# Turning both groups of the previous tile ahead of a descending tile's own products, and raising three step rates

## The chip, the cores and the metric

One core of one Trainium2 chip. The metric is the device time of one execution in microseconds (us). The kernel before takes 1788.37 us, the median of three runs from 1788.04 to 1789.47.

## What is computed

One layer of a hybrid encoder for two requests with shared weights, a sample of 1024 tokens and a prompt of 256, at model width 2048:

```
hn   = rms_norm(x, norm_g)
proj = hn @ w_in            # xbc, z_ssd, dt, q, k, v, z_att, mq, z_mem
# 1 SSD, 16 heads of 64 in two groups: forward and backward scan over chunks of 128 tokens
y_f  = ssd_scan(xs, dt[0], A[0], B, C)
y_b  = ssd_scan of the same, reversed in time
y    = y_f + y_b + d_skip * xs
o_ssd = rms_norm per group (y * silu(z_ssd))
# 2 attention within a window of 128 tokens, 8 heads, 2 key heads, a sink; gated by z_att
# 3 attention to a memory of 256 entries, 4 heads of 128; gated by z_mem
out  = x + concat(o_ssd, o_att, o_mem) @ w_out
```

All is float32. The step inside one backward chunk that matters here is `y_off = C @ S * exp(acs)`, then `S = S * decay + st`: each tile needs the state that the tile after it in time left behind.

## The kernel before

**Tiles.** The tokens are ten tiles of 128: tiles 0 to 7 are the sample, 8 and 9 the prompt. They are worked in two groups of five, 0 to 4 and 5 to 9. The big products run in blocks, one for a slice of 512 or 256 columns of a weight. A weight chunk is loaded by SP into one of four buffers (`wraw`), split into a high part by ACT (L206, `wh`) and a low part by VectorE (L207, `wl`), and used in three products (L258 to L260 for five tiles at once, `block_tok`; L293 to L295 for features by 320 tokens, `block_feat`). These are the main matmuls, into five PSUM banks called `acc`. TensorE runs them in the order in which they are written.

**Lanes.** All other work is generators in two queues ("lanes"). After each k of a block, `pump(rates)` adds the block's two rates to what each lane is owed and takes whole steps of the lanes by turns; a step is what a generator does up to its next `yield`. `RATES[1]` holds the pair of each block of the second group of tiles, (first lane, second lane); a `block_feat` uses half of it for each k. The first lane holds attention (`attn`) and memory attention (`mem_attn`), the second the ascending and the descending half of the SSD (`ssd_up`, `ssd_down`). `need` takes steps until a named generator is done. So the rates and the number of steps decide beside which main matmuls a step's instructions stand; the engines then run them in a fixed order, each engine its own.

**What the lanes share.** All their products use one pool of three PSUM banks by turns (`pr`, `pd`, `pz`, `pyb`, `psc`, `pms`, `pcb`, `pxs`, `pst` and others), whatever the lane. A new tile waits until the reader of the tile three before it has emptied the bank.

**The descending half.** `ssd_down` runs for tiles 7 to 0 and then 9 and 8. A tile's steps in the kernel before: a first step with its loads by SP (old output `yd`, gate `zd`, state `st`, the turned diagonal part `ydT`), three empty ones (eight more for tiles 7 and 9), then

- the norm of the tile that ran before it (`norm_ssd`, two L1001 on VectorE, which need that tile's `yrs` from POOL), and `diag_in(0)`: four transposes `pd` (L1046) and an add on VectorE (L1047);
- for each of two groups of 512 columns: for the first group of tiles 0 to 4 four transposes `pz` (L1060), then the product with the state `pyb` (L1063), five or six operations on VectorE (L1065 to L1073) and a square on ACT (L1070);
- after each group a step that turns the same group of the tile before (`turn_ssd`: four transposes `pr`, L1010, a copy `so` by ACT, L1012, and a store to `oT` by SP, L1013); after the first group with `diag_in(1)`.

`last_y` hands the output of one tile to the next. Tiles 0 and 8 have no follower and flush their own output at the end: three empty steps, the norm, two empty steps, and two turns.

**What follows from it.** Block `o` (output projection) reads `oT`: at its third k and at its sixth, `fill_direct` loads chunks (`chd`, L188, by SP) of what the SSD stored, and ACT (L200, `xH`) and VectorE (L201) split them. `zm` fills in the same way from the attention outputs (L197 and L198). The loads wait on SP for the stores' landing.

Of the kernel before, what the change touches and what calls it, by code (L numbers as in the profile page):

```python
# [30 lines left out]

RATES = ({'kv': (4.0, 1.0), 'z1': (2.2, 1.7)},
         {'kv': (1.5, 1.5), 'x': (2.1, 2.15), 'q': (2.25, 2.5), 'za': (2.15, 2.5), 'z0': (2.1, 2.5),
          'z1': (2.1, 2.55), 'mq': (2.0, 2.7), 'zm': (1.75, 2.75), 'o': (2.15, 2.4)})
FAR = 1e30

UNITS = (0, 8, 1, 9, 2, 10, 3, 11, 4, 12, 5, 13, 6, 7)
# [7 lines left out]
def hymba_encoder_kernel(  # L45
# [37 lines left out]
    def psum(name):  # L83
        return mix.tile([P, 512], F32, tag="mix", name=name)
# [37 lines left out]
    def rsqrt(dst, src, scale, n):  # L122
        G.tensor_scalar(out=dst, in0=src, scalar1=scale, scalar2=EPS, op0=ALU.mult, op1=ALU.add)
        G.tensor_tensor(out=dst, in0=dst, in1=mhalf[:, :n], op=ALU.pow)

    def hv(ap, n=8):
        return ap.rearrange("p (h d) -> p h d", h=n)

    def hb(ap, n, d):
        return ap.unsqueeze(2).broadcast_to([P, n, d])  # L130
# [673 lines left out]
    def wb(name, dtype=F32, shape=(P, 512)):  # L804
        return mp.tile(list(shape), dtype, tag="wb", name=name, bufs=WBB)
# [190 lines left out]
    def norm_ssd():  # L996

        if "y" in last_y:
            t, ys, rs = last_y.pop("y")
            for g in range(2):  # L1000
                V.tensor_scalar(out=ys[g], in0=ys[g], scalar1=rs[:, g:g + 1], scalar2=None, op0=ALU.mult)  # L1001
                last_y[g] = t, ys[g]

    def turn_ssd(g):

        if g in last_y:
            t, y = last_y.pop(g)
            ps = psum("pr")
            for j in range(4):
                T.transpose(ps[:, j * P:(j + 1) * P], y[:, j * P:(j + 1) * P], ident)  # L1010
            o = mp.tile([P, 512], F32, tag="rb", name="so", bufs=RBB)
            A.activation(o, ps, AF.Copy)  # L1012
            S.dma_start(oT_d[2 + g][t // 5][:, :, t % 5 * P:(t % 5 + 1) * P], hv(o, 4))  # L1013

    def ssd_down(t):
        first = t in (0, NS)
        last = t in (NS - 1, NT - 1)
        tok = slice(t * P, (t + 1) * P)
        ss = sm.tile([P, 2], F32, tag="s2", name="yss", bufs=4)
        if not last:  # L1020
            cc = mp.tile([P, 2, P], F32, tag="btok", name="cc", bufs=1)
            S.dma_start(cc, xbc_d[10:12, :, tok].rearrange("f p c -> p f c"))
        ld = []
        for g in range(2):
            c = slice(g * 512, (g + 1) * 512)

            y = mp.tile([P, 512], F32, tag="ya" if t % 2 else "rf", name="yd", bufs=2)
            S.dma_start(y, yp_d[t][:, c])
            if g == 0 and t < 5:
                z = mp.tile([P, 512], F32R, tag="xs", name="zd", bufs=2)  # L1030
                S.dma_start(hv(z.bitcast(F32), 4), yT_d[:, :, tok])
            else:
                z = mp.tile([P, 512], F32, tag="xs", name="zd", bufs=2)
                S.dma_start(z, z_d[g][t])
            st = None
            if not first:
                st = state[:, c] if last else wb("st2")
                S.dma_start(st, sb_d[t][:, c])
            d = mp.tile([P, 4, P], F32R, tag="rb", name="ydT", bufs=RBB)
            S.dma_start(d.bitcast(F32), yd_d[t][:, 4 * g:4 * g + 4, :])  # L1040
            ld.append((y, z, st, d))

        def diag_in(g):
            ps = psum("pd")
            for j in range(4):
                T.transpose(ps[:, j * P:(j + 1) * P].bitcast(F32R), ld[g][3][:, j, :], identr)  # L1046
            V.tensor_add(ld[g][0], ld[g][0], ps)  # L1047

        for _ in range(9 if last else 4):
            yield  # L1050
        norm_ssd()
        diag_in(0)
        yield
        for g in range(2):
            c = slice(g * 512, (g + 1) * 512)
            y, z, st, _ = ld[g]
            if g == 0 and t < 5:
                zr, z = z, psum("pz")
                for j in range(4):
                    T.transpose(z[:, j * P:(j + 1) * P].bitcast(F32R), zr[:, j * P:(j + 1) * P], identr)  # L1060
            if not last:
                pf = psum("pyb")
                T.matmul(pf, cc[:, g, :], state[:, c], start=True, stop=True)  # L1063
                y2 = wb("y3")
                V.tensor_mul(hv(y2), hv(pf), hb(eacs_all[:, t, 16 + 8 * g:24 + 8 * g], 8, 64))  # L1065
                V.tensor_add(y, y, y2)
            V.tensor_mul(y, y, z)
            if g == 0 and t < 5:
                z = wb("zq")
            A.activation(z, y, AF.Square, scale=0.5, accum_out=ss[:, g:g + 1])  # L1070
            if not first and not last:
                V.tensor_mul(hv(state[:, c]), hv(state[:, c]), hb(cd_all[:, t, 16 + 8 * g:24 + 8 * g], 8, 64))
                V.tensor_add(state[:, c], state[:, c], st)  # L1073
            yield
            turn_ssd(g)
            if g == 0:
                diag_in(1)
                yield
        rs = sm.tile([P, 2], F32, tag="s2", name="yrs", bufs=4)
        rsqrt(rs, ss, 1.0 / 512, 2)  # L1080
        G.tensor_scalar(out=rs, in0=rs, scalar1=0.5, scalar2=None, op0=ALU.mult)
        last_y["y"] = t, [x[0] for x in ld], rs
        yield
        if first:
            for _ in range(3):
                yield
            norm_ssd()
            yield
            yield
            for g in range(2):  # L1090
                turn_ssd(g)
                yield
# [358 lines left out]
    def refill_o(grp, when):  # L1451
        def f(k):
            if k not in when:
                return []
            q = when[k]
            need((attn, mem_attn, ssd_down, ssd_down)[q], range(grp * 5, grp * 5 + 5))
            return [part(fill_direct, q, j, oT_d[q][grp][:, j, :],
                         gain=None if q < 2 else vec[:, R_SG + 4 * (q - 2) + j:R_SG + 4 * (q - 2) + j + 1])
                    for j in range(4)]
        return f  # L1460
# [161 lines left out]
    tok("z0", w_in_rows("z0"), ev_gate(0, 5), grp=1)  # L1622
    tok("z1", w_in_rows("z1"), ev_gate(1, 5), grp=1)
    queue(1, ssd_down, range(7, -1, -1))
    queue(1, ssd_up, range(8, 10))
    queue(1, ssd_down, range(9, 7, -1))
    tok("mq", w_in_rows("mq"), ev_raw(mq_d, 5), grp=1)
    gate("zm", 1, refill_o(0, {3: 0, 7: 1}))
# [100 lines left out]
```

## Time and profile before

| | |
|---|---|
| median of three runs | 1788.37 us |
| the profiled execution | 1792.47 us |
| its span, first to last instruction | 1790.8 us |
| granted TensorE clock | 1.000 |
| TensorE matmul busy | 1776.3 us |
| TensorE weight loads busy | 1605.2 us |
| VectorE, ACT, POOL busy | 1246.8, 921.7, 549.3 us |

Rows of the profile give a start, a duration, the engine and line, and the tile written `<-` the tiles read; "[0.72 <-ACT so L1012]" is the idle of the engine before it and what ended that. Rows of the waits are "total us, times, longest". PE is TensorE's matmuls and PEld its weight loads, which may run under an earlier matmul; matmuls are pipelined and a matmul's end is modelled. Buffer numbers in the order of the program (`pr_14873`) belong to one tile; the lines there are those of the kernel shown, which in the new kernel are two or three higher behind the change.

### The profile page before, as it was taken

How to read it: one execution, taken by the hardware profiler on the slowest of the kernel's cores; microseconds unless marked ns; L12 is line 12 of the kernel's file. 1: busy time of each engine (PE TensorE's matmuls, PEld its weight loads, DVE VectorE, ACT ScalarE, POOL GpSimd, SP SyncE). 2: the span in 40 equal slices, each digit the busy share in tenths (PEclk: the TensorE clock that was granted, in tenths of full speed). 3: DMA queues.
4: the chain of work that ended last, by engine and by line, in shares of the span. 5: the costliest groups of instructions: out<-in, count | busy, mean ns of one | idle time of the engine just before them, and what ended most of it. 6: DMA issues, size and time to landing. Idle time of an engine off the chain costs nothing.

```text
span 1790.8 us, 31435 instructions
## 1 busy us (share of the span) xinstructions
PE 1776.3 (99%) x10838; PEld 1605.2 (90%) x10838; DVE 1246.8 (70%) x2358; ACT 921.7 (51%) x2049; POOL 549.3 (31%) x900
## 2 busy tenths in 40 slices
PE   9999999999999999999999999999999999999999
PEld 7788999999998989999889977877988888899999
DVE  5495788888858878777765676557677644766665
ACT  6554555555434766656454565544447533543332
POOL 0105799998810101010001010000100000057775
PEclk9999999999999999999999999999999999999999
DMA  8663544445446644453635644557777764744442
GB/s 283 198 185 118 146 147 137 146 144 168 123 140 208 187 140 133 147 164 104 188 117 181 187 150 152 170 161 250 225 231 237 239 192 143 223 150 143 148 142 77
DMA packets 208207, 301.12 MB, mean 168 GB/s; under 512 B 19568, under 2 KB 86192, under 8 KB 208048
## 3 DMA queue, kind: packets, MB, share of 16 engines
q1 hardware_dynamic: 207904, 299.06, 54.5%
q8 instruction: 85, 1.39, 0.3%
q14 instruction: 74, 0.61, 0.1%
q10 hardware_dynamic: 144, 0.06, 0.0%
HBM read 236.36 MB, written 62.69 MB: 167 GB/s over the span
## 4 chain that ended last, share of the span: by engine, by line
PE 79%; issue 6%; POOL 5%; DMA 5%; DVE 3%; ACT 2%; SPq 0%; POOLq 0%; ACTq 0%; DVEq 0%
PE acc L258 9%; PE acc L260 9%; PE acc L259 9%; PE acc L1238 6%; PE acc L1236 6%; PE acc L1237 6%; PE acc L293 5%; PE acc L295 5%; PE acc L294 5%; POOL ws L1208 3%; PE accm L1237 2%; PE accm L1236 2%; PE accm L1238 2%; PE po L673 1%; PE ppt L663 1%
## 5 line engine op out<-in xcount | busy, mean ns | idle before, releaser
L207 DVE TENSOR_TENSOR wl<-wraw,wh 128x512 fp32r<-128x512 f32 (+1 forms) x480 | 345.3, 721 | 241.3 <-ACT wh L206 234.0
L206 ACT ACTIVATE wh<-wraw 128x512 fp32r<-128x512 f32 (+1 forms) x480 | 292.0, 613 | 297.4 <-PE acc L260 138.6
L258 PE MATMUL acc<-wh,xH 128*128 128x512 f32 (+1 forms) x1088 | 419.0, 385 | 2.7 <-ACT mkr L420 1.3
L259 PE MATMUL acc<-wl,xH 128*128 128x512 f32 (+1 forms) x1088 | 410.1, 377 | 0.7 <-DVE wl L207 0.7
L260 PE MATMUL acc<-wh,xL 128*128 128x512 f32 (+1 forms) x1088 | 410.2, 377 | 0.0
L258 PEld LDWEIGHTS acc<-wh,xH 128*128 128x128 f32 x1088 | 204.4, 188 | 41.5 <-issue 3.6
L259 PEld LDWEIGHTS acc<-wl,xH 128*128 128x128 f32 x1088 | 204.5, 188 | 38.5 <-DVE wl L207 3.1
L260 PEld LDWEIGHTS acc<-wh,xL 128*128 128x128 f32 x1088 | 204.2, 188 | 36.9 <-issue 0.2
L293 PE MATMUL acc<-xH,wh 128*128 128x320 f32 x640 | 202.7, 317 | 0.0
L206 ACT ACTIVATE sh<-ws 128x384 fp32r<-128x384 f32 x176 | 91.3, 523 | 214.5 <-POOL ws L1208 117.4
L294 PE MATMUL acc<-xL,wh 128*128 128x320 f32 x640 | 198.8, 311 | 0.0
L295 PE MATMUL acc<-xH,wl 128*128 128x320 f32 x640 | 198.0, 309 | 0.0
L207 DVE TENSOR_TENSOR sl<-ws,sh 128x384 fp32r<-128x384 f32 x176 | 124.8, 712 | 104.3 <-ACT sh L206 101.8
L1208 POOL TENSOR_TENSOR ws<-wraw 128x128 f32<-128x128 f32 x176 | 114.1, 648 | 203.8 <-DMA wraw<-in_w_in_pairs_dram 87.7
L635 POOL COPY lg<-nsink 128x2 f32<-128x2 f32 x40 | 14.1, 351 | 377.6 <-PE ppt L663 219.8
L293 PEld LDWEIGHTS acc<-xH,wh 128*128 128x128 f32 x640 | 120.2, 188 | 2.6 <-issue 2.2
L294 PEld LDWEIGHTS acc<-xL,wh 128*128 128x128 f32 x640 | 120.3, 188 | 1.7 <-issue 1.4
L1208 POOL TENSOR_TENSOR ws<-wraw,ws 128x128 f32<-128x128 f32 x176 | 116.7, 663 | 13.8
L295 PEld LDWEIGHTS acc<-xH,wl 128*128 128x128 f32 x640 | 120.2, 188 | 0.6 <-issue 0.5
L1208 POOL TENSOR_TENSOR ws<-ws,wraw 128x128 f32<-128x128 f32 x176 | 116.9, 664 | 0.0
L1208 POOL TENSOR_TENSOR wraw<-wraw 128x128 f32<-128x128 f32 x176 | 111.9, 636 | 13.7
L362 DVE SCALAR_TENSOR_TENSOR c<-u,vec,c 128x638 f32<-128x638 f32 (+1 forms) x96 | 90.0, 938 | 9.0 <-ACT c L357 8.7
(437 smaller groups left out, 3943.3 us busy)
## 6 DMA issues: line engine op xcount, KB each, us to landing
wraw<-in_w_in_laid_dram SPq DMA_DIRECT2D x176, 256.0 KB, 2.9
wraw<-in_w_in_pairs_dram SPq DMA_DIRECT2D x112, 256.0 KB, 2.8
wraw<-in_w_out_laid_dram SPq DMA_DIRECT2D x64, 256.0 KB, 3.3
wraw<-in_w_out_pairs_dram SPq DMA_DIRECT2D x64, 256.0 KB, 2.8
rf<-ac SPq DMA_DIRECT2D x40, 256.0 KB, 4.1
rb<-ac SPq DMA_DIRECT2D x40, 256.0 KB, 4.9
wraw<-in_w_mem_laid_dram SPq DMA_DIRECT2D x32, 256.0 KB, 4.7
xst<-in_x_sample_dram SPq DMA_DIRECT2D x20, 256.0 KB, 4.7
```

Of the source, the lines that this page charges most:

```text
L206: a = A.activation(h, raw, AF.Copy)
L207: b = V.tensor_sub(l, raw, h.bitcast(F32))
L258: T.matmul(ps[t][:, :n], sh, h[:, :n], start=(k_ == 0), stop=False)
L259: T.matmul(ps[t][:, :n], sh, l[:, :n], start=False, stop=False)
L260: T.matmul(ps[t][:, :n], sl, h[:, :n], start=False, stop=(k_ == KT - 1))
L293: T.matmul(o, sh, cur["H", q][:, m, c], start=(k == 0), stop=False)
L294: T.matmul(o, sh, cur["L", q][:, m, c], start=False, stop=False)
L295: T.matmul(o, sl, cur["H", q][:, m, c], start=False, stop=(k == KT - 1))
L1208: G.tensor_tensor(out=o, in0=x, in1=y, op=op)
L1236: T.matmul(ps[p], h, xh, start=(k_ == 0), stop=False)
L1237: T.matmul(ps[p], h, xl, start=False, stop=False)
L1238: T.matmul(ps[p], l, xh, start=False, stop=(k_ == 7))
```

## The change

The turns move from behind each group to a step of their own, ahead of both groups and behind `diag_in(0)`. Three of the rate pairs of the second group of tiles change, so that the second lane takes more steps for each k. A tile then has one step more. Nothing that is computed changes.

```diff
-          'z1': (2.1, 2.55), 'mq': (2.0, 2.7), 'zm': (1.75, 2.75), 'o': (2.15, 2.4)})
+          'z1': (2.1, 2.55), 'mq': (1.95, 3.0), 'zm': (1.75, 3.05), 'o': (2.15, 2.5)})
...
         diag_in(0)
         yield
         for g in range(2):
+            turn_ssd(g)
+        yield
+        for g in range(2):
             c = slice(g * 512, (g + 1) * 512)
             y, z, st, _ = ld[g]
...
                 V.tensor_add(state[:, c], state[:, c], st)
             yield
-            turn_ssd(g)
             if g == 0:
                 diag_in(1)
                 yield
```

TensorE, where tile 4 of the descending half works: before, with the turn of tile 5's first group behind the first product,

```order
L1060 MATMUL pz_14858<-identr_84,zd_14739 128x128 x4
L1063 MATMUL pyb_14863<-state_6124,cc_14735 128x512
L1010 MATMUL pr_14873<-identr_84,yd_14504 128x128 x4
L293 MATMUL acc_14897<-xH0_6806,wh_14902 128x320
L294 MATMUL acc_14897<-xL0_6807,wh_14902 128x320
L295 MATMUL acc_14897<-xH0_6806,wl_14903 128x320
L1046 MATMUL pd_14881<-identr_84,ydT_14751 128x128 x4
```

and now:

```order
L1046 MATMUL pd_14829<-identr_84,ydT_14697 128x128 x4
L293 MATMUL acc_14908<-xH0_6806,wh_14914 128x320
L294 MATMUL acc_14908<-xL0_6807,wh_14914 128x320
L295 MATMUL acc_14908<-xH0_6806,wl_14915 128x320
L673 MATMUL po_14835<-pT_14675,v_all_6118 64x256 x4
L1010 MATMUL pr_14841<-identr_84,yd_14494 128x128 x4
L1010 MATMUL pr_14849<-identr_84,yd_14502 128x128 x4
L293 MATMUL acc_14909<-xH0_6806,wh_14914 128x320
L294 MATMUL acc_14909<-xL0_6807,wh_14914 128x320
L1063 MATMUL pz_14857<-identr_84,zd_14693 128x128 x4
L1066 MATMUL pyb_14862<-state_6124,cc_14689 128x512
```

Both turns (`pr`) stand together ahead of the first product. The second place is tile 0 in block `zm`, on TensorE: before,

```order
L1046 MATMUL pd_15782<-identr_84,ydT_15691 128x128 x4
L1060 MATMUL pz_15790<-identr_84,zd_15689 128x128 x4
L1063 MATMUL pyb_15795<-state_6124,cc_15685 128x512
L293 MATMUL acc_15402<-xH3_7438,wh_15805 128x320
L294 MATMUL acc_15402<-xL3_7439,wh_15805 128x320
```

and now:

```order
L1010 MATMUL pr_15788<-identr_84,yd_15390 128x128 x4
L1010 MATMUL pr_15796<-identr_84,yd_15398 128x128 x4
L1063 MATMUL pz_15804<-identr_84,zd_15677 128x128 x4
L293 MATMUL acc_15412<-xH3_7438,wh_15827 128x320
L294 MATMUL acc_15412<-xL3_7439,wh_15827 128x320
L1066 MATMUL pyb_15809<-state_6124,cc_15673 128x512
L1046 MATMUL pd_15819<-identr_84,ydT_15685 128x128 x4
```

The two turns of tile 1 moved here from 50 rows further down; `pd` of the first group went ahead by a step. Their copies on ACT stand here now:

```order
L197 ACTIVATE xH1_15781<-chd_15735 128x640
L197 ACTIVATE xH1_15781<-chd_15785 128x640
L206 ACTIVATE wh_15921<-wraw_15919 128x512
L722 ACTIVATE sq_15942<-mq_15940 128x512
L1012 ACTIVATE so_15793<-pr_15788 128x512
L1012 ACTIVATE so_15801<-pr_15796 128x512
```

In the old order a square of L1070 followed L722, and the two copies came seven rows later. The third place is ACT at the start of block `o`, where `wh` is a weight split, `mpr` the exps of memory attention and `xH2` the fill with the SSD's chunks: before,

```order
L206 ACTIVATE wh_16187<-wraw_16185 128x512
L754 ACTIVATE mpr_16039,mden_16040<-pms_16029,mm_16036,mr_15946 128x256 x2
L831 ACTIVATE cb_16055<-pcb_16046 128x256
L754 ACTIVATE mpr_16067,mden_16068<-pms_16057,mm_16064,mr_15946 128x256 x2
L200 ACTIVATE xH2_16109<-chd_15986,vec_200 128x640
```

and now:

```order
L206 ACTIVATE wh_16187<-wraw_16185 128x512
L200 ACTIVATE xH2_16109<-chd_15986,vec_200 128x640
L200 ACTIVATE xH2_16109<-chd_16026,vec_200 128x640
L200 ACTIVATE xH2_16109<-chd_16113,vec_200 128x640
L754 ACTIVATE mpr_16039,mden_16040<-pms_16029,mm_16036,mr_15946 128x256 x2
```

The first three fills now come ahead of the first pair of exps.

## The prediction

> **What bounds the kernel now.** I read the page first, then the windows around the descending tiles, then the waits of the matmul engine and of its weight loads there, and last the timelines of the two places that the change packs tighter.
>
> ```profile
> span 1790.8 us, 31435 instructions
> PE 1776.3 (99%) x10838; PEld 1605.2 (90%) x10838; DVE 1246.8 (70%) x2358; ACT 921.7 (51%) x2049; POOL 549.3 (31%) x900
> ```
>
> TensorE is the bound over the whole program: 1776.3 of 1790.8 us. The change adds no arithmetic, so it can only move the remaining idle. The next view cuts the part in which tiles 7 to 0 descend (blocks `mq`, `zm`, the start of `o`) and tiles 9 and 8 (1480 to 1520).
>
> ```profile
> core 0: us, PE busy (x) PEld busy (x) DVE busy (x) ACT busy (x) POOL busy (x), PEclk, DMA share, GB/s
> 1183.00:1242.00 59.00, 59.00 (x303) 45.38 (x301) 37.96 (x88) 26.71 (x67) 6.49 (x16) 1.00 0.59 184
> 1242.00:1327.00 85.00, 83.80 (x570) 74.88 (x568) 64.39 (x128) 38.71 (x92) 9.79 (x21) 1.00 0.72 224
> 1327.00:1360.00 33.00, 31.45 (x172) 25.88 (x171) 23.79 (x48) 21.11 (x51) 1.11 (x3) 1.00 0.92 288
> 1360.00:1480.00 120.00, 119.85 (x660) 100.64 (x659) 69.25 (x138) 60.06 (x144) 5.36 (x8) 1.00 0.67 213
> 1480.00:1520.00 40.00, 40.00 (x189) 32.25 (x188) 15.03 (x26) 12.69 (x25) 2.23 (x6) 1.00 0.48 140
> ```
>
> First column minus the first busy column: PE idles 0, 1.20, 1.55, 0.15 and 0 us, 2.90 us in 337. What ends these waits, first on PE, then on its weight loads (a waiting matmul's load waits too, and may have waited under a running matmul):
>
> ```profile
> PE pst L868 <- ACT fh L882: 1.6, 1, 1.6
> PE pyb L1063 <- ACT so L1012: 0.7, 1, 0.7
> PE pd L1046 <- DVE nm L643: 0.5, 1, 0.5
> PEld pr L1010 <- ACT so L1012: 1.8, 3, 0.6
> PEld pst L868 <- ACT fh L882: 1.8, 1, 1.8
> PEld pyb L1063 <- ACT so L1012: 1.2, 2, 0.9
> PEld pd L1046 <- DVE nm L643: 0.9, 1, 0.9
> ```
>
> The four load rows sum to 1.8 + 1.8 + 1.2 + 0.9 = 5.7 us. So what the old order loses lies between 2.9 us (idle that PE's rows show) and 5.7 us (all load waits lost). All four are waits for a bank of the three-bank pool or for what stands ahead on ACT.
>
> **The change part by part.** The counts stay: 20 copies `so` of 0.59 us in the stretch, with four transposes each.
>
> ```profile
> L1012 ACT ACTIVATE so<-pr 128x512 f32<-128x512 f32 x20 | 11.7, 590 | 8.5 <-PE pr L1010 7.2 <-ACT so L1012 0.8 <-ACT lg L647 0.5
> L1001 DVE TENSOR_SCALAR yd<-yd,yrs 128x512 f32<-128x512 f32 x20 | 9.0, 485 | 18.0 <-POOL yrs L1081 18.0
> ```
>
> *Removed.* The old order sets a `pr` between a tile's two products (tile 4 in the first place shown with the change), and the next `pyb` needs a bank whose `so` may stand behind something else on ACT. Now both turns stand ahead of both products, and the second `pyb` no longer follows a turn. Tile 4 before:
>
> ```profile
> 1245.22 0.60 PE L1010 MATMUL pr<-identr,yd 128*128 128x128 f32 x4
> 1247.64 1.13 PE L1063 MATMUL pyb<-state,cc 128*128 128x512 f32 x2 [0.72 <-ACT so L1012]
> 1246.47 0.63 ACT L602 ACTIVATE sq<-q 128x512 f32<-128x512 f32 x1 [2.33 <-DMA q<-q]
> 1247.01 0.58 ACT L1012 ACTIVATE so<-pr 128x512 f32<-128x512 f32 x1
> ```
>
> Here `so` sat behind L602, which waited 2.33 us for a DMA; that pairing is gone. I count all old waits as gone and price the new ones apart: −3.5 us, nearer the 2.9 of PE's own rows than the 5.7, because a load's wait under a running matmul costs nothing.
>
> *Norm and turn in one pump.* In tiles 5, 4 and 2 the norm (two L1001 of 0.485 us) and the turns now fall in one pump, so `pr` can wait for the second L1001: 0 to 0.5 us each, 0 to 1.5 together. Main matmuls stand between in most; I take +0.5.
>
> *Tiles 2 and 1 beside attention of tile 9.* Their `pr`, `pz`, `pyb`, `pd` now share the three banks with scores in the same pump, at three points where a product's bank is released only by L643's reduction. The nearest row is `pd` behind `nm`: 0.5 on PE, 0.9 on the load. Three of these: 0 to 2.7; three of 0.45 make +1.3.
>
> *Tile 0's group in `zm`.* In the second place shown, `pr`, `pr`, `pz` (which fill the three banks), two main matmuls, `pyb_15809` and `pd` now follow each other. `pyb_15809` waits for `so_15793`, and on ACT that copy stands behind two L197 (fills of xH1), a weight split and L722. Before, the turns stood 50 rows later on PE, and the engines ran this place so:
>
> ```profile
> 1318.51 0.74 ACT L197 ACTIVATE xH<-chd 128x640 fp32r<-128x640 f32 x1 [4.63 <-DMA chd<-oT]
> 1319.15 0.62 ACT L206 ACTIVATE wh<-wraw 128x512 fp32r<-128x512 f32 x1
> 1319.67 0.62 ACT L722 ACTIVATE sq<-mq 128x512 f32<-128x512 f32 x1
> 1317.87 0.46 PE L1046 MATMUL pd<-identr,ydT 128*128 128x128 f32 x4
> 1318.16 0.51 PE L1060 MATMUL pz<-identr,zd 128*128 128x128 f32 x4
> 1318.50 1.09 PE L1063 MATMUL pyb<-state,cc 128*128 128x512 f32 x2
> 1326.04 0.31 PE L293 MATMUL acc<-xH,wh 128*128 128x320 f32 x1
> 1326.18 0.31 PE L294 MATMUL acc<-xL,wh 128*128 128x320 f32 x1
> 1340.33 0.63 ACT L206 ACTIVATE wh<-wraw 128x512 fp32r<-128x512 f32 x1 [2.56 <-issue]
> ```
>
> The load that L197 waited for ended at 1318.51 and the wait hid, since no PE work there hung on ACT. If the last chunk lands as late again, ACT is through L722 at 1319.67 + 0.62, plus a second L197 (0.64 to the next start) = 1320.9, and `so` ends at 1321.5. PE is there at 1317.87 + three transposes of 0.3 + two matmuls of 0.15 = 1319.1. So 0 (landing 2.4 us earlier) to 2.4; the only row there is speaks for late: +1.5. On SP the two stores of these copies now stand ahead of the store of a gate and of `wraw_16185`; SP waits there for `so`, but the split of that weight ran at 1340.33 before, 19 us on, so this is nothing.
>
> *The start of `o`.* Tile 0's own turns come 10 main matmuls earlier (after 20 of the block, not 30). What hangs on them is two stores, four chunk loads that SP issues once the stores have landed, and the fills xH2 on ACT. In the third place shown, three of these fills went ahead of the memory softmax's exps, which free the bank that `pxs` takes 12 main matmuls after `pcb`.
>
> ```profile
> 1332.48 0.39 PE L260 MATMUL acc<-wh,xL 128*128 128x512 f32 x1
> 1332.70 0.39 PE L258 MATMUL acc<-wh,xH 128*128 128x512 f32 x1
> 1336.82 1.78 SPq L1013 DMA_DIRECT2D oT<-so  x2
> 1341.83 1.74 SPq L188 DMA_DIRECT2D chd<-oT  x4
> DMA to landing us min/median/max: 5.3/5.7/6.4
> 1342.80 0.57 ACT L754 ACTIVATE mpr<-pms,mm,mr 128x256 f32<-128x256 f32 x1 [1.84 <-DVE mm L750]
> 1342.16 0.39 PE L258 MATMUL acc<-wh,xH 128*128 128x512 f32 x1
> 1343.90 0.38 ACT L831 ACTIVATE cb<-pcb 128x256 f32<-128x256 f32 x1
> 1347.17 1.62 ACT L200 ACTIVATE xH<-chd,vec 128x640 fp32r<-128x640 f32 x2 [1.80 <-DMA chd<-oT]
> L200 ACT ACTIVATE xH<-chd,vec x4: 813/824/832, 1347.2 to 1349.9; 128x640 fp32r<-128x640 f32 x4
> ```
>
> Matmuls step by 0.22 us, so the stores go out 2.2 us earlier, at 1334.6. Issue of store to issue of load took 5.0 us, the load 5.3 (the row is the loads' own): landing 1344.9. Three fills of 0.82 and two exps (1342.80 to 1343.90: 1.1 us) end at 1348.5. PE comes to `pxs` at about 1344.9 (before, `pcb` and the scores were done by 1342.16; 12 × 0.22 more): 3.6 us of wait. The `fh` ahead of `pst` comes after another fill and may add 0.9. So 0 to 4.5; I take +2.5, below the worked 3.6, because both landing times were taken at a DMA share of 0.92, which may be lower 2 us earlier. It is nothing if the chunks land by 1341.3.
>
> The Trainium skill (DMA: Bandwidth & Descriptors, "Anatomy of one DMA — SWDGE (gpsimd) path", so for DMAs that GpSimd issues, and these are SP's) gives a DMA a fixed 2 us or so plus bytes over 436 GB/s, which for these 320 KB is an estimated 2.7 us. By that the chunks would be in before 1341.3, this term would be 0 and the sum −0.2. The trace disagrees: 5.3 to 6.4 us, at a DMA share of 0.92.
>
> *Rates and the rest.* The larger second rates pay for one step more a tile; tile 8 ends before the drain instead of in it. That stretch shows 0 idle: 0.
>
> Sum: −3.5 + 0.5 + 1.3 + 1.5 + 2.5 = +2.3 us. The profiled execution took 1792.47 us, 1.67 outside its span and 4.1 above the median of 1788.37; 1794.8 against it, or **1790.7 us** against the median.
>
> **The rivals.** A measurement of this kernel can tell about 0.2%, 3.6 us, from no change.
>
> *ACT in its order holds PE: slower (0.37).* The two fill places come out at the upper ends. −2.9 + 0.5 + 1.3 + 2.4 + 4.5 = +5.8: 1794.2 us; with the other two at theirs, +8.2. It decides if chunks land later than 1318.5 in `zm` or 1344 in `o`. For it: the two DMA waits of 4.63 and 1.80 us on ACT at these places. Against: the new turns change what SP issues, so landings may move. The Trainium skill (Perfetto Trace Analysis, "Matmuls") asks that independent matmul groups rotate through PSUM banks so that one is emptied under the next; five tiles in a row on three banks go against it. The old trace shows that wait only once on PE, 0.7 us.
>
> *The waits just go: faster (0.15).* No new stall, −2.9 to −5.7 us, middle −4.3: 1784.1. For it: most old waits are a `pr` between products, which is what the order removes. Against: the fills ahead of the exps stand in the order, whatever lands when.
>
> *Waits change places, no net (0.13).* Old and new within 1 us of each other: 1788.4. For it: nearly every wait is 0.5 to 0.7 us, one copy long.
>
> **How the numbers follow.** The forecast has 0.35. All of it but a sixth (0.06, slower) lies within 3.6 us; of the slower rival 0.05 and of the faster 0.02 fall within it too. Within 0.2%: 0.29 + 0.13 + 0.05 + 0.02 = 0.49; slower: 0.06 + 0.32 = 0.38; faster: 0.13. The range goes from 1784.6 (in the faster case) to 1796.0 (just under all upper ends, 1796.6).
>
> **What would show it.** Right: in the new trace no `pyb` behind `so` near tile 4; `pyb` of tile 0 waiting for `so` with L197 on a DMA ahead of it; `pxs` in `o` waiting for an exp of L754 with L200 ahead; the idle between 1183 and 1520 rising from 2.9 to about 5. Wrong: chunk loads that land under 4 us in `o` (then nothing or a gain); PE idle in the window below 2; or time lost outside it, say in the drain or where weights wait on SP behind the stores.

## The result: slower by 0.24%

The changed kernel takes 1793.33 us, the median of 13 runs (1790.31 to 1795.53); the kernel before, in 13 runs beside it, 1788.43. The ratio is 1.0024, 95% interval 1.0017 to 1.0031: +4.3 us (3.0 to 5.5). Slower, inside the range, and just past the 0.2% up to which the forecast had counted "no change".

The two profiled executions hide it: their spans are 1790.8 us before and 1790.3 now. The one of before had lost 4.2 us ahead of the descending tiles, where the programs do the same: one of the last matmuls that both run in the same order starts at 1181.94 us there and at 1177.71 now (PE idle 4.7 us in its first 400 us, 2.6 now). From that matmul to one behind the stretch (1664.02 and 1663.58), where the orders agree again, the changed kernel takes 3.8 us more. So the stretches are compared. The same windows as in the prediction, for the changed kernel, with two slices of 3 us added:

```profile
1183.00:1242.00 59.00, 58.98 (x306) 45.97 (x304) 37.31 (x85) 26.92 (x65) 7.29 (x16) 1.00 0.66 203
1242.00:1327.00 85.00, 83.54 (x558) 74.37 (x557) 64.91 (x130) 38.27 (x91) 9.33 (x21) 1.00 0.72 224
1327.00:1360.00 33.00, 29.37 (x154) 24.44 (x153) 21.42 (x43) 21.04 (x50) 1.11 (x3) 0.95 0.85 256
1343.00:1346.00 3.00, 0.56 (x5) 0.56 (x5) 2.39 (x6) 3.00 (x7) 0.00 (x0) 0.93 0.84 234
1346.00:1349.00 3.00, 3.00 (x11) 2.31 (x10) 2.73 (x9) 2.86 (x10) 0.00 (x0) 0.50 0.90 281
1360.00:1480.00 120.00, 119.94 (x664) 100.92 (x663) 70.29 (x139) 59.20 (x143) 5.53 (x8) 1.00 0.68 213
1480.00:1520.00 40.00, 40.00 (x186) 32.56 (x186) 16.02 (x28) 12.66 (x24) 2.23 (x6) 1.00 0.46 137
```

PE's idle in the five large windows is 0.02 + 1.46 + 3.63 + 0.06 + 0 = 5.17 us, against 2.90 before. And one thing is new: the granted clock (third number from the end) is 0.95 in the third window. PE stands nearly still for 2.4 us from 1343, and in the next slice the clock is 0.50. What PE's matmuls waited for in the stretch:

```profile
PE pxs L861 <- ACT mpr L754: 2.5, 1, 2.5
PE pr L1010 <- DVE yd L1001: 1.1, 1, 1.1
PE pr L1010 <- DVE yd L1047: 0.9, 1, 0.9
PE pyb L1066 <- ACT so L1012: 0.3, 1, 0.3
```

The old `pst`, `pd` and most of `pyb` are gone; `pxs` behind an exp is the largest. The chain of work that ended last runs through that place without a break, from tile 0's last square to the half clock (start, duration, what; its main rows):

```profile
1328.17 0.73 ACT zd L1073 x2
1329.26 0.71 POOL yrs L124
1330.30 0.50 DVE yd L1001
1330.93 1.06 PE pr L1010 x8
1332.22 4.32 DMA oT<-so
1336.92 5.70 DMA chd<-oT
1342.64 0.87 ACT xH L200 x2
1344.20 1.20 ACT mpr L754 x4
1345.44 0.68 PE pxs L861 x4
1346.67 0.43 PE acc L259
1349.53 0.23 PE acc L259
```

The turns, a store of 4.3 us, chunk loads of 5.7, the fills, the exps, and only then `pxs`; main matmuls then step by 0.43 us instead of 0.23.

### The profile page after: what moved, and what is told of

It is laid out like the page before. It is cut to its first block, busy times and chain, and to the rows that moved or that the text cites. A ratio compares the mean times of both kernels' runs of the same rounds, so it can differ in the third digit from the quotient of the medians.

```text
span 1790.3 us, 31456 instructions
## 1 busy us (share of the span) xinstructions
PE 1776.5 (99%) x10838; PEld 1606.3 (90%) x10838; DVE 1247.4 (70%) x2358; ACT 922.8 (52%) x2049; POOL 542.0 (30%) x900
## 4 chain that ended last, share of the span: by engine, by line
PE 86%; issue 6%; DMA 3%; DVE 2%; ACT 1%; POOL 1%; SPq 0%; ACTq 0%; DVEq 0%; POOLq 0%
PE acc L258 10%; PE acc L259 10%; PE acc L260 10%; PE acc L1238 7%; PE acc L1240 7%; PE acc L1239 7%; PE acc L293 5%; PE acc L295 5%; PE acc L294 5%; PE accm L1239 3%; PE accm L1238 3%; PE accm L1240 3%; PE po L673 1%; PE ppt L663 1%; PE py L942 1%
## 5 line engine op out<-in xcount | busy, mean ns | idle before, releaser
L1210 POOL TENSOR_TENSOR ws<-wraw 128x128 f32<-128x128 f32 x176 | 110.5, 628 | 207.3 <-DMA wraw<-in_w_in_pairs_dram 88.7
```

The source lines that it names most:

```text
L1210: G.tensor_tensor(out=o, in0=x, in1=y, op=op)
```

## The experiments

Theory A: the loss is that one place, the fills ahead of the exps and the clock behind the wait. Theory B: five tiles in a row on three banks cost a little at every descending tile. Theory C: the raised rates. All runs are of one core; each ratio is to the kernel before on the same chip. Idle is PE's in 1183 to 1520 of one profiled execution, from the windows as above. "Clock" counts timed runs whose mean granted clock was 0.999 or less.

| kernel | ratio (95%) | median us | idle us | clock |
|---|---|---|---|---|
| before | 1 | 1787.6 to 1789.1 | 2.90 | 2 of 84 |
| changed, first series | 1.0024 (1.0017 to 1.0031) | 1793.33 | 5.17 | 7 of 13 |
| changed, again | 1.0026 (1.0017 to 1.0036) | 1793.18 | 6.04 | 7 of 10 |
| exps first | 1.0006 (0.9997 to 1.0015) | 1790.13 | 3.20 | 1 of 11 |
| two fills ahead | 1.0026 (1.0017 to 1.0036) | 1793.41 | 4.37 | 6 of 9 |
| one fill ahead | 1.0024 (1.0015 to 1.0034) | 1792.71 | 5.82 | 3 of 11 |
| turns only | 1.0018 (1.0009 to 1.0027) | 1792.66 | 5.65 | 3 of 11 |
| rates only | 1.0007 (0.9999 to 1.0016) | 1790.63 | 5.02 | 4 of 11 |
| exps first, one step behind the norm | 1.0012 (1.0003 to 1.0020) | 1791.92 | 3.56 | 0 of 11 |
| exps first, two steps ahead of it | 1.0006 (0.9997 to 1.0016) | 1788.40 | 2.77 | 1 of 11 |
| before, fh first | 0.9999 (0.9990 to 1.0008) | 1788.82 | 2.26 | 0 of 11 |
| before, fh and so first | 1.0000 (0.9991 to 1.0010) | 1788.17 | 0.86 | 0 of 11 |

**The changed kernel again**, unedited.

> The changed kernel itself, as the anchor of this chip: 1.0024 of the kernel before, so about +4.3 us, by every theory.

As expected. Its profile repeats the place, with `pxs` waiting 2.7 us and `pyb` 1.2.

**The exps ahead of the fills.** One edge on ACT; nothing else moves up to there, while behind it some splits, `fh` and later fills change places on ACT and VectorE too. `last_exp[0]` is the second exp of the second pair of tile 5.

```diff
-            A.activation(h, ch, AF.Copy, scale=gain)
+            with ExitStack() as st:
+                if q == 2 and j >= 0 and last_exp[0] is not None:
+                    st.enter_context(tc.issue_after(last_exp[0]))
+                A.activation(h, ch, AF.Copy, scale=gain)
```

> The changed kernel with one edge: in block o the four fills of xH2 on ACT stand behind the exps of memory attention's tile 5 (as they do in the kernel before). Theory A (the fills ahead of the exps hold PSUM banks; the 2.5 us wait of pxs and the 3.3 us at half clock behind it, 1.65 us, are nearly the whole loss): the wait of pxs goes, the clock stays at 1.00, and the time falls by about 4 us against the changed kernel, to within 1.5 us of the kernel before. Theory B (five tiles in a row on three banks cost a little at each descending tile): at most the 2.5 us of this one wait come back, the rest of the loss stays, +2 us or more. Theory C (the raised rates): as B.

What PE waited for in the stretch:

```profile
PE pr L1016 <- DVE yd L1007: 1.1, 1, 1.1
PE pms L751 <- DVE mql L736: 0.9, 1, 0.9
PE pr L1016 <- DVE yd L1053: 0.9, 1, 0.9
```

`pxs` is gone, the clock is 1.00 in every window, and the ratio falls from 1.0026 to 1.0006; the intervals don't overlap. Some 3.6 of 4.7 us of the loss hang on this order of instructions on ACT. That is theory A; B and C keep at most the rest, whose interval holds zero. How the 3.6 us divide between the wait, the half clock and what else moves behind the edge is not shown.

**Two fills ahead, one fill ahead.** The same edge, behind the first pair of exps, for the fills from the third (and, in the second kernel, `j >= 1`, from the second). Against the kernel with the exps first:

```diff
-                if q == 2 and j >= 0 and last_exp[0] is not None:
+                if q == 2 and j >= 2 and last_exp[0] is not None:
```

> The changed kernel with two instead of three fills ahead of the first pair of exps. A fill takes 0.82 us, so pxs waits about 1.7 instead of 2.5 us. If the halved clock belongs to the wait alone and has a threshold between the 1.7 us that the kernel before shows at full clock and the 2.5 us here: no slice at 0.50, 0.8 + 1.65 = about 2.4 us faster than the changed kernel, +2 us against the kernel before. If the halved clock has another cause or a lower threshold: only 0.8 us faster, +3.5 us.

> One fill ahead of the first exps instead of three (the changed kernel) or two (1.6 us of wait in its profile, full clock there, but 6 of its 9 timed runs at a mean clock of 0.999). With one the wait of pxs is some 0.8 us at most. If runs of 0.999 are those in which this wait passes some 1.8 us: hardly a run at 0.999, no slice at half clock, and +1.5 us against the kernel before (the remainder that exps_first shows, +1.1, and 0.4). If the clock's drop has nothing to do with this wait: about half the runs at 0.999 and +3 us or more.

Neither gain came out: the times fit the second branch of each expectation (+3.5 us lies inside the first interval, and +3 or more came in the second, though with 3 of 11 runs at the lower clock and not half). With two, the profiled execution showed 1.6 us and full clock, but the timed runs were no faster than the changed kernel and 6 of 9 showed the clock. With one, `pxs` still waited 2.4 us in the profile. ACT and VectorE there:

```profile
1344.36 0.83 ACT L204 ACTIVATE xH<-chd,vec 128x640 fp32r<-128x640 f32 x1 [2.81 <-DMA chd<-oT]
1346.29 0.56 ACT L758 ACTIVATE mpr<-pms,mm,mr 128x256 f32<-128x256 f32 x1 [1.10 <-DVE mm L754]
1345.22 0.88 DVE L205 SCALAR_TENSOR_TENSOR xL<-chd,vec,xH 128x640 fp32r<-128x640 f32 x1 [2.35 <-ACT xH L204]
1346.02 0.15 DVE L754 SCALAR_TENSOR_TENSOR mm<-mm,mr 128x2 f32<-128x2 f32 x1
```

The first fill alone waits 2.8 us for its chunk; the exps behind it then wait for `mm` on VectorE, which stands behind the low half `xL` of that very fill. So the fills' number alone does not set the wait. The landing of the chunks does as well, and it differs from one execution to the next: ACT waited 2.0, 3.1, 2.0 and 2.8 us for the first one in the four profiles (changed, again, two ahead, one ahead), and in the changed kernel another 1.0 for the second. Between the two profiles with 2.0, one fill fewer goes with 0.9 us less wait of `pxs` (2.5 and 1.6), near the 0.82 that had been priced; the pricing left out the landing and VectorE. Against the timed runs neither can be weighed: 0.8 us is less than half the width of their intervals.

**Half of the change at a time.** The new turn place with the old rates, against the changed kernel:

```diff
-          'z1': (2.1, 2.55), 'mq': (1.95, 3.0), 'zm': (1.75, 3.05), 'o': (2.15, 2.5)})
+          'z1': (2.1, 2.55), 'mq': (2.0, 2.7), 'zm': (1.75, 2.75), 'o': (2.15, 2.4)})
```

and the same lines the other way round in the kernel before (rates only).

> The turns moved as in the change, the rates left as before. Its order at the start of o has the exps ahead of the fills. Theory A: no wait of pxs, the time within 1.5 us of the kernel before. Theory B: the packed turns cost by themselves, +3 us or more. Theory C (rates): within 1 us of the kernel before.

> The raised rates with the turns where they were. In its order at the start of o the fills of xH2 stand ten rows ahead of the exps on ACT, behind turns that come earlier still. Theory A (the loss is one place, where fills wait for chunks ahead of exps): no wait of pxs for an exp, so within 1.5 us of the kernel before. Theory C (the rates by themselves run the second lane ahead of its data): +3 us or more. Theory D (each new order of steps against main matmuls deals its own hand of waits, of 2 to 5 us in sum): anything from -1 to +4, with other waits than those of the kernel before.

Neither half has the wait of `pxs`, yet turns only costs 1.0018. Its waits, and then those of rates only:

```profile
PE pz L1063 <- DVE oT L676: 1.9, 2, 1.2
PE pst L868 <- ACT fh L882: 1.8, 1, 1.8
PE pr L1010 <- DVE yd L1001: 0.8, 1, 0.8
PE ppt L663 <- DVE nm L643: 0.8, 1, 0.8
```

```profile
PE pd L1046 <- DMA ydT<-yd: 1.7, 1, 1.7
PE pst L868 <- ACT fh L882: 1.5, 1, 1.5
PE pmt L767 <- DVE mpr L759: 0.9, 1, 0.9
PE ppt L663 <- DVE oT L676: 0.5, 1, 0.5
PE pyf L885 <- ACT cb L831: 0.3, 1, 0.3
```

With the old rates, `pz` behind two turns finds the third bank still held by attention's output (theory B's wait, 1.9 us at two places), and `pst` is as late as before. With the new rates and the old place, the load of a turned diagonal arrives 1.7 us late. Expectation A (within 1.5 us) held for the rates and failed for the turns: the packed turns can cost by themselves, but at other places than in the changed kernel. What fits both is theory D, written for the second: each alignment of steps against main matmuls brings its own two or three waits of 1 to 2 us. With its range of −1 to +4 us it could hardly fail, so it is a description and not shown as a cause.

**The rest of the loss.** Empty steps in tile 0's flush, with the exps first: two more ahead of the norm (first diff), or one behind it (second).

```diff
-            for _ in range(3):
+            for _ in range(5):
                 yield
             norm_ssd()
```

```diff
             norm_ssd()
             yield
             yield
+            yield
             for g in range(2):
                 turn_ssd(g)
```

> The kernel with the exps ahead of the fills, and one more empty step between tile 0's norm and its two turns. In the profiles of the changed kernel, and of the one with exps first, pr waits 1.1 us there for the norm on VectorE. If that wait is real loss: it goes, and the time is 1.1 us under exps_first, level with the kernel before. If the later stores give it back (chunks land later, fills and fh behind them): level with exps_first, with a wait of pst for fh in its place.

> The kernel with the exps ahead of the fills, and two more empty steps ahead of tile 0's norm, so that the norm and both of its turns come later in block o (one more step behind the norm, in exps_n3, had moved the second turn alone and left the 1.1 us of pr for the norm). If those 1.1 us are the rest of the loss: the wait is gone and the time is 1.1 us under exps_first, level with the kernel before (0.999 to 1.001). If the rest lies at other places (pr behind L1047 in tile 1, pms behind mql, pd behind so): 1.0006 as for exps_first.

The step behind the norm moved only the second of the two turns, and the 1.1 us stayed: it tells nothing on the question. The two ahead of it removed them (idle 3.20 to 2.77 us), but the ratio stayed at 1.0006. One microsecond is under what one such series resolves, so whether that wait is part of the rest is open. That there is a rest is likely: the three kernels with the exps first stand at 1.0006, 1.0012 and 1.0006, and the interval of the second leaves out 1.

**A version that might beat both.** On the kernel before: the last two fills behind `fh` of tile 8; then also the square L602 behind `so` of tile 5. Both with the same kind of edge (`last_exp[0]` is here `fh`, `last_so[0]` the copy):

```diff
-            A.activation(h, ch, AF.Copy, scale=gain)
+            with ExitStack() as st:
+                if q == 2 and j >= 2 and last_exp[0] is not None:
+                    st.enter_context(tc.issue_after(last_exp[0]))
+                A.activation(h, ch, AF.Copy, scale=gain)
...
-        A.activation(sq, q, AF.Square)
+        with ExitStack() as st:
+            if t == 9 and last_so[0] is not None:
+                st.enter_context(tc.issue_after(last_so[0]))
+            A.activation(sq, q, AF.Square)
```

> The kernel before, with the last two fills of xH2 behind the fh of tile 8 on ACT, so that pst does not stand behind all four. If pst's 1.6 us there is loss: it falls to 0.3 or less and the time falls by about 1.3 us, 0.9993 of the kernel before. If something else is late next there (the fills themselves, which main matmuls read from the eighth k): no change, or slower.

> The kernel before with the two fills behind fh (before_fh2), and the square L602 of attention tile 9, which waits 2.3 us for its DMA, behind the copy so of tile 5 on ACT. pyb's wait for so near tile 4 (0.7 to 1.1 us) goes as well: PE idle in the stretch falls from 2.9 to about 1.2 us, and the time by 1.7 to 2.4 us, 0.9987 to 0.999. If what these waits cost is hidden in slack elsewhere: no change.

The waits went nearly as meant. With the first edge alone `pst` waits 0.2 us and `pyb` 1.1, and the ratio is 0.9999 where 0.9993 had been expected. With both edges PE waits for this in the whole stretch:

```profile
PE pd L1058 <- DVE nm L651: 0.5, 1, 0.5
PE pst L877 <- DVE fl L900: 0.2, 1, 0.2
PE pmt L775 <- DVE mpr L767: 0.2, 1, 0.2
```

Idle falls from 2.90 to 0.86 us. The time does not follow: 1.0000, interval 0.9991 to 1.0010, which just leaves out the 0.9989 that 2.0 us would give. It beats the changed kernel and is not told apart from the kernel before. In its profiled execution the gain is there: between the same two matmuls as in the result it takes 2.6 us less than that of before. So one of the two profiled executions does not stand for the timed runs, or the waits differ from run to run; which, is not shown.

## Why the prediction was right, step by step

**The bound and the main mechanism held.** PE's idle moved, and it rose from 2.90 to 5.17 us where "about 5" had been forecast. The place worked out from rows of before, the start of `o`, is the one that decided.

- *Removed (−3.5).* `pst`, `pd` and the `pyb` of tile 4 no longer wait: −2.8 of PE's 2.9 (the `pyb` of 0.3 us is a new one, at tile 0). The end near PE's own rows was right; −3.5 was more than these rows had to give.
- *Norm and turn in one pump (+0.5).* No PE wait at tiles 5, 4 or 2. The same wait appeared at tile 0's own turns, 1.1 us, which the sum did not have: the flush came nearer to the square, POOL and VectorE (the first three rows of the chain) than its steps allow.
- *Tiles 2 and 1 (+1.3).* One wait, 0.9 us, at tile 1, for L1047 and not L643. The row was the right size; three was too many.
- *Tile 0 in `zm` (+1.5).* The order did what was said. ACT waited 3.1 us there for the chunk, and `pyb` 0.3 us in this execution, 0.9 in its second profile, 1.2 with one fill ahead, 0.3 or less in the other kernels with this order. Between the bounds; the value was too high for the profiled one:

```profile
1313.05 1.54 ACT L197 ACTIVATE xH<-chd 128x640 fp32r<-128x640 f32 x2 [3.08 <-DMA chd<-oT]
1315.53 1.06 ACT L1012 ACTIVATE so<-pr 128x512 f32<-128x512 f32 x2
1316.16 1.12 PE L1066 MATMUL pyb<-state,cc 128*128 128x512 f32 x2
```

- *The start of `o` (+2.5).* The wait was 2.5 us. The rule of the Trainium skill (DMA: Bandwidth & Descriptors, "Anatomy of one DMA — SWDGE (gpsimd) path"), by which the term would have been 0, was set aside rightly: the chain shows 4.3 us for the store and 5.7 for the chunk. The worked 3.6 was high: the loads could go out 4.3 us after the stores and not 5.0 as before, and ACT could start on the first chunk 4.3 us after its load was issued (1336.55 to 1340.81) where 5.3 had been taken; the second chunk then held it for another 1.0.
- *Rates and the rest (0).* The stretch from 1480 to 1520 shows 0 idle in both kernels, and nothing was lost behind it.
- **The term that was mis-sized is this last one, by what follows the wait.** The working stopped at PE's return. The clock then stood at half for some 3.3 us: 33 us at a mean of 0.95 are 1.65 us lost. With it, idle and clock give 5.17 − 2.90 + 1.65 = +3.9 us, against 3.8 between the same two matmuls of the two profiles and the +4.3 measured (3.0 to 5.5). Not every timed run has the half clock: by the runs counted at the end it is worth about 1.1 us on average, so part of what the forecast lacked is not placed.

That the sum's +2.3 and the idle's 5.17 − 2.90 = 2.27 agree so well is luck. Term by term the errors are about +0.7 (removed), −0.5 (norm), +1.1 (the flush), −0.4, −1.2 and 0 us, and they cancel; the second profile of the same kernel has 6.04 us of idle.

Of the rivals, "ACT in its order holds PE" named the mechanism and put it at +5.8; the truth lies between it and the forecast. The likeliest class, within 0.2%, missed by 0.04%, and the interval (from 0.17%) still reaches into it. "The waits just go" fell, though the old waits did go. "Waits change places" describes PE's rows, which are other ones than before, but not the time: they grew.

## What to carry to other kernels

Where an engine runs in its order, look at what an earlier store triggers: a load that lands 10 us later ends in an instruction that may now stand ahead of one that frees a PSUM bank, and it takes VectorE's half of the work with it. Moving such an instruction behind the urgent ones was worth some 3.6 us here, with the turns left in their new place. Count PE's longest single wait apart from the sum of the waits, since the clock can make it dearer; and below 0.1% or so believe the timed runs rather than the idle of one profiled execution: rates only shows 3.2 us more than before between the two matmuls of its profile, and 1.3 (−0.2 to 2.9) in the timed runs.

## What the runs showed of the hardware

In five of the twelve profiles the granted clock falls to half, once each in the middle of the program: for 3.41 us, behind a wait of PE. Half of that, 1.7 us, is lost by it, as an estimate. By the clock records of a trace, the changes lie whole multiples of 3.41 us apart (in the changed kernel 393, 1 and 129 of them). So the trace can be cut into pieces of that length. In the changed kernel, the piece with the wait, the one at half clock and the next (columns as in the windows above: length, PE busy first, the clock third from the end):

```profile
1342.19:1345.61 3.42, 0.90 (x6) 0.44 (x4) 2.78 (x9) 2.97 (x7) 0.00 (x0) 1.00 0.90 278
1345.61:1349.02 3.41, 3.41 (x14) 2.72 (x13) 3.14 (x10) 3.27 (x10) 0.00 (x0) 0.50 0.86 263
1349.02:1352.43 3.41, 3.41 (x20) 2.88 (x20) 3.02 (x7) 2.60 (x8) 0.00 (x0) 1.00 0.98 254
```

With rates only, where `pd` waits 1.7 us for a load:

```profile
1249.49 0.51 PE L1046 MATMUL pd<-identr,ydT 128*128 128x128 f32 x4 [1.68 <-DMA ydT<-yd]
1247.17:1250.58 3.41, 1.73 (x16) 1.26 (x13) 1.81 (x4) 0.15 (x1) 0.00 (x0) 1.00 0.98 355
1250.58:1254.00 3.42, 3.42 (x10) 2.42 (x10) 1.99 (x5) 0.63 (x1) 0.00 (x0) 0.50 0.81 256
```

And with two fills ahead, where the clock stays:

```profile
1340.79:1344.20 3.41, 1.80 (x11) 1.26 (x10) 2.76 (x8) 3.00 (x7) 0.00 (x0) 1.00 0.94 316
1344.20:1347.61 3.41, 3.41 (x19) 2.70 (x19) 3.41 (x11) 3.41 (x11) 0.00 (x0) 1.00 0.84 291
```

PE's idle in the piece ahead of the half clock is 2.52 us (changed), 2.36 (again), 1.90 (one fill ahead), 1.81 (turns only) and 1.68 (rates only). The largest that left the clock at full are 1.61 (two fills ahead) and 1.55 (before; the expectation for two fills took 1.7 for that wait). So in these twelve executions the border lies near half a piece, and what counts is the idle within one piece: of the 2.4 us wait with one fill ahead only 1.90 fall into the piece ahead of the drop. The pieces lie elsewhere in each execution: `pxs` begins to wait 0.7 us after a piece's start in the changed kernel's first profile and 3.1 us after it in the second. A wait that such a border cuts in two may therefore leave the clock alone; no profile here shows that for a wait over 1.7 us.

The half clock does not come in every run. Of the changed kernel's 23 timed runs 14 show a mean clock of 0.999 or less, with a median of 1793.8 us; the other 9 have 1792.0. The difference is near the 1.7 us of the profile, though longer waits may themselves be in the slower group; over all 23 runs it comes to 14/23 of 1.8, an estimated 1.1 us. It is the smaller part of the loss, for the 9 are still 3.4 us above the kernel before (1788.4 and 1788.7 beside them). Nor does the count follow the ratios elsewhere: with rates only the 4 runs at 0.999 are no slower than the other 7 (medians 1790.3 and 1790.6). The Trainium skill (TensorE: Matmul & The Clock Gate, "Part 1: The HAM clock gate") has a window of 3.4 us that runs free of the kernel, after which an idle array drops to half its clock; the 3.41 us agree with that length, and so do the borders that lie elsewhere in each execution, but here a window that was half idle was enough. The same page ("HAM oscillation — how this bites in real kernels") warns of idle gaps over 3.4 us; here 1.7 was enough.
